# First feed-forward of a Conformer layer: one more pair of tiles by seven products, five sums by DMA, another head and another end

## The chip, the cores and the metric

The kernel runs on one core of one Trainium2 chip. The metric is the device time of one execution in microseconds (us); smaller is better. Before the change it is 2106.32 us, the median of three runs (2105.33 to 2113.24).

The engines are TensorE (PE in the profile, PEld where it loads weights), VectorE (DVE), ScalarE (ACT), GpSimd (POOL) and SyncE (SP). SP issues most of the DMA transfers; ACT and POOL issue a few. Each engine works through its own list of instructions in order.

## The reference, cut to what matters

One layer on 256 tokens of 2048 features, in float32:

```python
def swiglu_ffn(h, w_in, w_out):
    gate, up = jnp.split(h @ w_in, 2, axis=-1)
    return (jax.nn.silu(gate) * up) @ w_out
...
h = rms_norm(x, ffn1_norm[l])
x = x + MACARON_SCALE * swiglu_ffn(h, ffn1_w_in[l], ffn1_w_out[l])
# then: convolution and spatial gating, cross-attention
h = rms_norm(x, ffn2_norm[l])
x = x + MACARON_SCALE * swiglu_ffn(h, ffn2_w_in[l], ffn2_w_out[l])
return rms_norm(x, final_norm)
```

`w_in` is 2048 x 11264 (5632 gate columns and 5632 up columns), `w_out` 5632 x 2048.

## The kernel before

**Numbers in two parts.** To keep float32 accuracy, each operand of a large product is split into a high part (rounded to fp32r by a cast on ACT) and a low part (the difference, by a subtraction on DVE). A product is then three matmuls: high x high, high x low, low x high. All large matmuls are 128 x 128 x 512. A tile of weights is 128 x 1024 floats, 512 KB: `raw` as loaded, `hl` as split.

**The first feed-forward** is the class `FeedForward`. The 11264 columns of `w_in` are cut into 11 groups `j` of 512 gate and 512 up columns; a group runs over 16 tiles `k` of 128 input features. Group 0 (`run`, first loop) handles one tile after the other with 12 matmuls each (`by_two`), while x arrives: `x_arrives` loads two tiles of x, multiplies by the gain and splits (`gained`, L239 and L240), and `x_more` loads x once more by rows and squares it (`x_squares`, L525) for the root of the mean square, which `give` needs when the group ends.

Groups 1 to 10 (`group`) take the tiles in eight pairs. A pair marked "C" in `PATTERNS` takes eight products of half-tiles (`eight`: 24 matmuls). A pair marked "S" takes seven (`seven`: 21 matmuls), for which DVE first makes sums of weight halves (L388, L389, L394, L401), and the splits are those of the sums (`parts`: cast L339 on ACT, subtraction L340 on DVE). The sums on the x side (`sides`) are made once, in group 0. Before the change the pattern is "SCSCSCCC".

**Sums by DMA.** For the tiles listed in `SUMMED` (2, 7 and 13 of each group) DVE does not subtract. `summed` lets ACT write minus the high part into the low half of a buffer (L358), then the high part (L359), and POOL issues a DMA that loads the weights a second time and adds them to that low half (L360):

```python
nc.scalar.activation(out=hl[:, 1], in_=raw, func=AF.Copy, scale=-1.0)
nc.scalar.copy(out=hl[:, 0], in_=raw)
nc.gpsimd.dma_start(out=hl[:, 1], in_=self.w_in[j, :, k], accum_op=ALU.add)
```

There are two such buffers in the first feed-forward, used by turns: `hl_s`, and the second half of `more` (which lies where x lay, and is there from the end of group 0). The buffer for the sum after next is refilled right after a summed tile has been used, so a refill begins when TensorE has read the low half for the last time (L289 reads it) and must have landed when TensorE reads it next. In the second feed-forward there is one buffer, `hl_s`.

**Order.** The program is written in one order and a scheduler with a model of times sets the order on each engine; the matmuls of neighbouring tiles stand interleaved there. A DMA is issued when its buffer is free; nine raw buffers go round (`raw`).

**The end.** The last 512 columns of the output are added, squared (`add_up`) and scaled by the inverse root (`give`), token half by token half, and stored.

Of the kernel before, what the change touches and what calls it, by code (L numbers as in the profile page):

```python
# [36 lines left out]
PATTERNS = ("SCSCSCCC", "SCSCSCCC")  # L37

SUMMED = ((2, 7, 13), (2, 7, 13))
# [3 lines left out]
    ("ffn1_norm", KD), ("mix_norm", KD), ("xattn_norm", KD), ("mem_norm", KD), ("ffn2_norm", KD),  # L43
# [23 lines left out]
def layer(ctx: ExitStack, tc: tile.TileContext, a: dict):  # L67
# [118 lines left out]
    nc.vector.memset(ones, 1.0)  # L186
    nc.scalar.activation(out=st.tile([P, 1], F32, name="warm"), in_=ones[:, 0:1], func=AF.Silu)
    ident = const.tile([P, P], F32, name="ident")
    make_identity(nc, ident)
    pv = const.tile([P, NPV], F32, name="pv")  # L190
    xt = ctx.enter_context(tc.tile_pool(name="xt", bufs=1))
    xT = xt.tile([P, KD, T], F32, name="xT", tag="x")
# [44 lines left out]
    def gained(dst, k, x, g):  # L237

        nc.scalar.activation(out=dst[:, k, 0], in_=x, func=AF.Copy, scale=g)  # L239
        nc.vector.scalar_tensor_tensor(  # L240
            out=dst[:, k, 1], in0=x, scalar=g, in1=dst[:, k, 0].bitcast(F32), op0=ALU.mult, op1=ALU.subtract
        )

# [55 lines left out]
    class FeedForward:  # L299
# [62 lines left out]
        def sides(self, i):  # L362
# [4 lines left out]
            for q in range(2):  # L367
                nc.scalar.activation(out=xg[:, q], in_=xT[:, k + q], func=AF.Copy, scale=col(self.gain, k + q))
# [55 lines left out]
        def group(self, j, r, after=()):  # L424
# [10 lines left out]
            for p, c in enumerate(self.pattern):  # L435
# [8 lines left out]
                else:  # L444
                    late = p > self.spairs[-1] and len(after) > 0
                    self.eight(j, p, b, p == self.pattern.index("C"), p == n - 1, late)
                    if p > self.spairs[-1] + 1:
# [7 lines left out]
        def run(self, before, after, root, more=None):  # L455
# [3 lines left out]
            for k in range(KD):  # L459
                before(k)  # L460
                w = self.parts(self.raw(0, k))
# [3 lines left out]
                if k == 13:  # L465
                    r = root()
                    nc.scalar.activation(out=st.tile([P, 1], F32, name="warm"), in_=ones[:, 0:1], func=AF.Silu)
                    self.summed(0)
            if more is not None:
                more()  # L470
                self.summed(1)
            self.give(0, [acc[t][0] for t in range(2)], [acc[t][1] for t in range(2)], r)
            turns = [self.turn(i) for i in range(2 * NG)]
            for j in range(1, NG):
                if j < NG - 1:
                    self.group(j, r)
                else:
                    now, turns = turns[:4], turns[4:]
# [40 lines left out]
    head = PV["mix_norm"][0]  # L519

    def x_squares(c):

        raw = wraw.tile([P, 1024], F32, name="raw")
# [3 lines left out]
    with ExitStack() as stack:  # L527
        ff = FeedForward(stack, ("S1", "S0", "S2"), x_hl, "ffn1_norm", a["ffn1_w_in"], PATTERNS[0], SUMMED[0])

        def x_arrives(k):  # L530
            if k % 2 == 0:
                nc.sync.dma_start(out=xT[:, k:k + 2], in_=a["xT"][:, k:k + 2])
            if k == 0:
                nc.sync.dma_start(out=pv[:, :head], in_=a["pv"][:, :head])
            gained(x_hl, k, xT[:, k], col("ffn1_norm", k))

        def x_more(k):
            if k == 6:
                nc.sync.dma_start(out=pv[:, head:], in_=a["pv"][:, head:])
            if k in (5, 7, 9, 11):  # L540
                x_squares(k // 2 - 2)
            if k in (6, 9, 12):
# [13 lines left out]
        turns = ff.run(x_arrives, x_more, x_root, x_given)  # L556
# [588 lines left out]
```

## Time and profile before

| what | value |
|---|---|
| median of three runs | 2106.32 us |
| the profiled execution: its own time | 2108.84 us |
| the profiled execution: span from first to last instruction | 2107.0 us |
| mean granted TensorE clock | 0.998 |
| TensorE busy | 2084.5 us, 99% of the span, 9764 matmuls |
| DVE busy | 1576.8 us, 75% |
| ACT busy | 1161.6 us, 55% |
| first matmul starts | 7.11 us |
| first matmul of group 1 | 57.53 us |
| first matmul of the down projection | 475.06 us |

Read a row of the timeline so: start, duration, engine, line of the kernel, operation, output<-inputs; in brackets how long the engine sat idle before it, and what ended that. Matmuls overlap (one lasts 0.39 us, but they follow each other every 0.23 us), so the pace is a stretch divided by its matmuls.

### The profile page before, as it was taken

The page shows a single profiled execution, that of the slowest core. Times are in us where ns is not written, and L with a number is a line of the kernel's source. Part 1 is how long each engine was busy: PE and PEld are TensorE (multiplying, and loading weights), DVE is VectorE, ACT ScalarE, POOL GpSimd, SP SyncE. Part 2 cuts the span into 40 slices and gives each one's busy share as a digit, 9 for nine tenths or more (in the row PEclk, how much of TensorE's full clock was granted, in tenths as well). Part 3 has the DMA queues.
Part 4 walks back from the last instruction along what each step waited for, and adds up shares of the span by engine and source line. Part 5 has one row for each costly group of instructions (what it writes and reads, how often), then busy time and mean ns, then how long its engine had stood idle before and what let it go on. Part 6 is the DMA issues. An engine that isn't in the chain of part 4 may idle for free.

```text
span 2107.0 us, 26590 instructions
## 1 busy us (share of the span) xinstructions
PE 2084.5 (99%) x9764; PEld 1738.5 (83%) x9764; DVE 1576.8 (75%) x2215; ACT 1161.6 (55%) x1450; POOL 67.7 (3%) x83
## 2 busy tenths in 40 slices
PE   8999999999999999999999999999999999999998
PEld 6888888888888888888888888888888888888886
DVE  6888888876655589889877665777888887787754
ACT  7666566645544454445665454556665666554443
POOL 0000000000000000000000000000000000000000
PEclk9999999999999999999999999999999999999999
DMA  9778777855666676666565543686787778556664
GB/s 360 230 227 257 229 238 245 263 167 169 216 198 188 206 236 200 190 176 185 176 201 185 186 154 111 206 281 191 231 259 247 232 229 250 178 160 202 197 192 149
DMA packets 122244, 442.34 MB, mean 210 GB/s; under 512 B 13697, under 2 KB 13825, under 8 KB 121729
## 3 DMA queue, kind: packets, MB, share of 16 engines
q1 hardware_dynamic: 113184, 407.35, 58.8%
q0 software_dynamic: 8640, 32.51, 8.5%
q8 instruction: 76, 1.25, 0.2%
q10 hardware_dynamic: 288, 0.79, 0.1%
q14 instruction: 56, 0.45, 0.1%
HBM read 438.49 MB, written 2.10 MB: 209 GB/s over the span
## 4 chain that ended last, share of the span: by engine, by line
PE 84%; issue 11%; DMA 2%; ACT 1%; POOL 1%; DVE 1%; SPq 0%; POOLq 0%; ACTq 0%
PE acc L172 12%; PE acc L173 12%; PE acc L171 12%; PE acc L125 9%; PE acc L289 7%; PE acc L288 7%; PE acc L291 7%; PE acc L126 4%; PE acc L277 2%; PE acc L276 2%; PE acc L275 2%; PE aux L263 1%; PE acc L1066 1%; PE acc L1065 1%; PE acc L1067 1%
## 5 line engine op out<-in xcount | busy, mean ns | idle before, releaser
L113 DVE TENSOR_TENSOR hl<-raw,hl 128x1024 fp32r<-128x1024 f32 (+1 forms) x402 | 488.6, 1216 | 282.5 <-ACT hl L112 281.1
L112 ACT CAST hl<-raw 128x1024 fp32r<-128x1024 f32 (+1 forms) x402 | 419.7, 1045 | 481.6 <-PE acc L173 289.3
L339 ACT CAST hl<-spare 128x1024 fp32r<-128x1024 f32 (+1 forms) x135 | 131.8, 993 | 95.5 <-DVE spare L389 38.5
L340 DVE TENSOR_TENSOR hl<-spare,hl 128x1024 fp32r<-128x1024 f32 (+1 forms) x135 | 154.4, 1150 | 35.8 <-ACT hl L339 34.2
L288 PE MATMUL acc<-hl,x_hl 128*128 128x512 f32 x408 | 144.2, 394 | 9.7 <-ACT hl L339 9.7
L289 PE MATMUL acc<-hl,x_hl 128*128 128x512 f32 x408 | 149.9, 395 | 0.0
L340 DVE TENSOR_TENSOR hl<-raw,hl 128x1024 fp32r<-128x1024 f32 (+1 forms) x101 | 113.9, 1131 | 45.9 <-ACT hl L339 44.3
L339 ACT CAST ring<-spare 128x1024 fp32r<-128x1024 f32 (+1 forms) x99 | 97.2, 988 | 68.9 <-DVE spare L389 26.9
L340 DVE TENSOR_TENSOR ring<-spare,ring 128x1024 fp32r<-128x1024 f32 (+1 forms) x99 | 112.9, 1145 | 19.9 <-ACT ring L339 18.8
L291 PE MATMUL acc<-hl,x_hl 128*128 128x512 f32 x408 | 127.5, 392 | 0.0
L339 ACT CAST hl<-raw 128x1024 fp32r<-128x1024 f32 (+1 forms) x101 | 97.7, 977 | 51.8 <-PE acc L291 16.1
L172 PE MATMUL acc<-hl,x_hl 128*128 128x512 f32 x256 | 100.5, 392 | 0.2 <-DVE hl L113 0.2
L172 PE MATMUL acc<-hl,m_hl 128*128 128x512 f32 x256 | 100.4, 392 | 0.0
L173 PE MATMUL acc<-hl,m_hl 128*128 128x512 f32 x256 | 100.2, 391 | 0.0
L173 PE MATMUL acc<-hl,x_hl 128*128 128x512 f32 x256 | 99.8, 390 | 0.0
L288 PEld LDWEIGHTS acc<-hl,x_hl 128*128 128x128 f32 x408 | 76.8, 189 | 25.9 <-ACT hl L339 10.1
L289 PE MATMUL acc<-ring,x_hl 128*128 128x512 f32 x248 | 93.1, 389 | 0.0
L288 PE MATMUL acc<-ring,x_hl 128*128 128x512 f32 x248 | 91.2, 390 | 0.0
L171 PE MATMUL acc<-hl,m_hl 128*128 128x512 f32 x256 | 91.2, 393 | 0.0
L289 PEld LDWEIGHTS acc<-hl,x_hl 128*128 128x128 f32 x408 | 77.2, 190 | 16.9 <-DVE hl L340 1.1
L291 PEld LDWEIGHTS acc<-hl,x_hl 128*128 128x128 f32 x408 | 77.5, 190 | 16.4
L125 PE MATMUL acc<-x_hl,hl 128*128 128x512 f32 x256 | 91.0, 398 | 0.0
(359 smaller groups left out, 5173.9 us busy)
## 6 DMA issues: line engine op xcount, KB each, us to landing
spare<-in_ffn_w_in SPq DMA_DIRECT2D x192, 512.0 KB, 6.4
raw<-in_ffn_w_out SPq DMA_DIRECT2D x176, 512.0 KB, 3.8
raw<-in_ffn_w_in SPq DMA_DIRECT2D x160, 512.0 KB, 6.3
hl_s<-in_ffn_w_in POOLq DMA_DIRECT2D x44, 512.0 KB, 7.3
raw<-in_w_mix_vg SPq DMA_DIRECT2D x32, 512.0 KB, 4.6
raw<-in_w_k SPq DMA_DIRECT2D x32, 512.0 KB, 4.0
raw<-in_w_v SPq DMA_DIRECT2D x32, 512.0 KB, 4.4
raw<-in_w_mix_out SPq DMA_DIRECT2D x32, 512.0 KB, 4.6
```

What stands on the lines that cost most here:

```text
L112: nc.scalar.copy(out=hl[:, 0, :size], in_=raw[:, :size])
L113: newest[0] = nc.vector.tensor_tensor(out=hl[:, 1, :size], in0=raw[:, :size], in1=hl[:, 0, :size].bitcast(F32), op=ALU.subtract)
L125: nc.tensor.matmul(acc, lhsT=w_hi, rhs=x_hl, start=first, stop=False, skip_group_check=True)
L126: nc.tensor.matmul(acc[:, 0], lhsT=w_lo, rhs=x_hl[:, 0], start=False, stop=last, skip_group_check=True)
L171: nc.tensor.matmul(acc[t], lhsT=x[:, 0, s], rhs=hi[:, k], start=k0 + k == 0, stop=False)
L172: nc.tensor.matmul(acc[t], lhsT=x[:, 0, s], rhs=lo[:, k], start=False, stop=False)
L173: nc.tensor.matmul(acc[t], lhsT=x[:, 1, s], rhs=hi[:, k], start=False, stop=k0 + k == nk - 1)
L288: nc.tensor.matmul(acc[t][g], lhsT=x[:, 0, s], rhs=hi[:, cols[g]], start=(t, g) in first, stop=False)
L289: nc.tensor.matmul(acc[t][g], lhsT=x[:, 0, s], rhs=lo[:, cols[g]], start=False, stop=False)
L291: nc.tensor.matmul(acc[t][g], lhsT=x[:, 1, s], rhs=hi[:, cols[g]], start=False, stop=last)
L339: nc.scalar.copy(out=hl[:, 0, :n], in_=raw[:, :n])
L340: newest[0] = nc.vector.tensor_tensor(out=hl[:, 1, :n], in0=raw[:, :n], in1=hl[:, 0, :n].bitcast(F32), op=ALU.subtract)
```

## The change

1. In the first feed-forward the pattern becomes "SCSCSCSC": pair 6 (tiles 12 and 13) goes by seven products. The summed tiles become 2, 6, 7, 11, 14; in the last group those below 14.
2. The head: the gain and tile 0 of x are one array (`gains_x0`), loaded with tile 1 of x from ACT's queue; the first weights come in two halves from SP (`early`) and are split half by half; 11 matmuls of ones by ones (`WARM`) precede the first real one. The rows of x go to `h` tiles that are still unused (not to `raw` buffers) and are asked for after tiles 2, 4, 6, 8 instead of 5, 7, 9, 11. The other constants (`pv`) come in one load.
3. `give(0)` is written ahead of `more()`. Of the turns of `h` for the down projection two stand in the last group instead of four.
4. The end: the sum of the first three squares is made ahead (`most`), so that `give` needs no reduction, and one operation with two scalars from a tile replaces a scalar_tensor_tensor.

```diff
-PATTERNS = ("SCSCSCCC", "SCSCSCCC")
-SUMMED = ((2, 7, 13), (2, 7, 13))
+PATTERNS = ("SCSCSCSC", "SCSCSCCC")
+SUMMED = ((2, 6, 7, 11, 14), (2, 7, 13))
+WARM = 11
...
+    gx = xt.tile([P, KD + KD * T], F32, name="gx", tag="x")
+    gains, xT = gx[:, :KD], gx[:, KD:].rearrange("p (k t) -> p k t", t=T)
+    nc.scalar.dma_start(out=gx[:, :KD + T], in_=a["gains_x0"])
+    nc.scalar.dma_start(out=xT[:, 1], in_=a["xT"][:, 1])
+    nc.vector.memset(ones, 1.0)
+    idle = pa.tile([P, 2, T], F32, name="aux")
+    for _ in range(WARM):
+        nc.tensor.matmul(idle[:, 0, :P], lhsT=ones, rhs=ones, start=True, stop=True)
...
+        def early(self, before):
+            self.raw_at += 1
+            self.at += 1
+            raw = wraw.tile([P, 1024], F32, name="raw")
+            hl = whl.tile([P, 2, 1024], F32R, name="hl")
+            halves = [slice(G, 2 * G), slice(0, G)]
+            for s in halves:
+                nc.sync.dma_start(out=raw[:, s], in_=self.w_in[0, :, 0, s])
+            x = before(0)
+            for s in halves:
+                with tc.issue_after(x.ins):
+                    split(hl[:, 0, s], hl[:, 1, s], raw[:, s])
+            return hl
...
+            self.give(0, [acc[t][0] for t in range(2)], [acc[t][1] for t in range(2)], r)
             if more is not None:
                 more()
                 self.summed(1)
-            self.give(0, [acc[t][0] for t in range(2)], [acc[t][1] for t in range(2)], r)
...
-                    now, turns = turns[:4], turns[4:]
+                    at = 2 * self.pattern[-2:].count("C")
+                    now, turns = turns[:at], turns[at:]
...
-        raw = wraw.tile([P, 1024], F32, name="raw")
+        raw = ff.h[7 - c].rearrange("p a b -> p (a b)")
...
-            if k in (5, 7, 9, 11):
-                x_squares(k // 2 - 2)
-            if k in (6, 9, 12):
+            if k in (2, 4, 6, 8):
+                x_squares(k // 2 - 1)
+            if k in (6, 9, 12, 15):
                 ff.sides(k // 3 - 2)
...
-            nc.vector.reduce_sum(out=tot, in_=sums[:, t], axis=AX.X)
-            nc.scalar.activation(out=s, in_=tot, func=AF.Sqrt, scale=1.0 / D, bias=eps)
+            nc.scalar.activation(out=s, in_=last, func=AF.Sqrt, scale=1.0 / D, bias=most[t])
...
-            nc.vector.scalar_tensor_tensor(out=r, in0=v, scalar=r, in1=s, op0=ALU.mult, op1=ALU.add)
+            nc.vector.tensor_scalar(out=r, in0=v, scalar1=r, scalar2=s, op0=ALU.mult, op1=ALU.add)
```

What this does to the order is seen at three places. In these rows `acc` and `aux` are accumulators, `hl`, `ring`, `more` and `hl_s` buffers of split weights, `x_hl` the split x.

**ACT at the start.** Before, ACT begins with its table and then waits for SP's loads of `xT` and `pv`:

```order
L187 ACT_TABLE_LOAD
L187 ACTIVATE warm<-ones 128x1
L467 ACTIVATE warm<-ones 128x1 x2
L239 ACTIVATE x_hl<-xT,pv 128x256 x2
L368 ACTIVATE spare<-xT,pv 128x256 x2
L339 CAST hl<-raw 128x1024
```

Now it issues two loads itself, and the first cast is of half a tile, after one tile of x:

```order
L196 DMA gx<-in_gains_x 128x272
L197 DMA gx<-in_xT 128x256
L204 ACT_TABLE_LOAD
L204 ACTIVATE warm<-ones 128x1
L499 ACTIVATE warm<-ones 128x1
L252 ACTIVATE x_hl<-gx 128x256
L123 CAST hl<-raw 128x512
```

Two tiles of x and two extra copies of x that stood ahead of the first cast have moved behind it.

**TensorE in a late group, from the last use of `hl_s` to its next.** The low half is read by L289 (before) and L303 (now). Before, the last reads of one content of `hl_s` and what follows:

```order
L289 MATMUL acc<-hl_s,x_hl 128x512
L288 MATMUL acc<-hl_s,x_hl 128x512
L289 MATMUL acc<-hl_s,x_hl 128x512
L291 MATMUL acc<-hl_s,x_hl 128x512 x2
L288 MATMUL acc<-ring,x_hl 128x512
```

and the first reads of the next content, 115 matmuls after the last L289 above:

```order
L291 MATMUL acc<-ring,x_hl 128x512 x2
L288 MATMUL acc<-hl_s,x_hl 128x512
L289 MATMUL acc<-hl_s,x_hl 128x512
L288 MATMUL acc<-hl_s,x_hl 128x512
L289 MATMUL acc<-hl_s,x_hl 128x512
```

Now, at about the same group, the last read of the low half:

```order
L302 MATMUL acc<-hl_s,x_hl 128x512
L303 MATMUL acc<-hl_s,x_hl 128x512
L305 MATMUL acc<-hl_s,x_hl 128x512
L302 MATMUL acc<-ring,x_hl 128x512
L303 MATMUL acc<-ring,x_hl 128x512
```

and the first read of the next content of the low half, 28 matmuls later:

```order
L302 MATMUL acc<-hl_s,x_hl 128x512 x3
L289 MATMUL acc<-ring 128x512
L289 MATMUL aux<-ring 128x512
L289 MATMUL acc<-hl,x_hl 128x512
L303 MATMUL acc<-hl_s,x_hl 128x512 x2
```

The two uses of one buffer have moved from 115 matmuls apart to 28.

**ACT in the same groups.** Before, two refills follow each other with seven casts between them:

```order
L358 ACTIVATE hl_s<-spare 128x1024
L359 CAST hl_s<-spare 128x1024
L339 CAST hl<-spare 128x512
L339 CAST ring<-spare 128x1024
L339 CAST more<-raw 128x1024
L339 CAST hl<-raw 128x1024
L339 CAST hl<-raw 128x512
L339 CAST hl<-raw 128x1024
L339 CAST ring<-spare 128x1024
L358 ACTIVATE more<-raw 128x1024
L359 CAST more<-raw 128x1024
```

Now three refills (two of `more`, one of `hl_s` between them) stand within twelve rows:

```order
L372 ACTIVATE more<-spare 128x1024
L373 CAST more<-spare 128x1024
L353 CAST ring<-raw 128x512
L432 ACTIVATE h_129<-spare,r_x_109 128x512
L353 CAST more<-raw 128x1024
L372 ACTIVATE hl_s<-spare 128x1024
L373 CAST hl_s<-spare 128x1024
L353 CAST hl<-spare 128x1024
L432 ACTIVATE h_129<-spare,r_x_109 128x512
L353 CAST hl<-spare 128x1024 x2
L372 ACTIVATE more<-raw 128x1024
L373 CAST more<-raw 128x1024
```

The refills, which were spread evenly, now come close together.

Over the program there are 8430 matmuls of 512 columns instead of 8460, and 49 refills in the first feed-forward instead of 29.

More of the change, by code (lines that the diff above doesn't have):

```diff
@@ L554, in x_given @@
             ff.hls.append(more[:, 2:])
-        turns = ff.run(x_arrives, x_more, x_root, x_given)
+        turns = ff.run(x_arrives, x_more, x_root, x_given, early=True)
         xT = xt.tile([P, KD, T], F32, name="xT", tag="x")
@@ L1050, in layer @@
         finish()
+        most = [st.tile([P, 1], F32, name=f"f_most{t}") for t in range(2)]
+        for t in range(2):
+            nc.vector.reduce_sum(out=most[t], in_=sums[:, t, 0:3], axis=AX.X)
+            nc.vector.tensor_scalar(
+                out=most[t], in0=most[t], scalar1=1.0 / D, scalar2=RMS_EPS, op0=ALU.mult, op1=ALU.add
+            )
         warm = nc.scalar.activation(out=st.tile([P, 1], F32, name="warm"), in_=ones[:, 0:1], func=AF.Sqrt)
```

45 lines of the change are left out of this document (22 added, 23 removed).

## The prediction

> **What bounds the kernel now.** I read the page's busy times first, then the busy times of three stretches of the first feed-forward, then the timeline where TensorE waits.
>
> ```profile
> PE 2084.5 (99%) x9764; PEld 1738.5 (83%) x9764; DVE 1576.8 (75%) x2215; ACT 1161.6 (55%) x1450; POOL 67.7 (3%) x83
> PE 84%; issue 11%; DMA 2%; ACT 1%; POOL 1%; DVE 1%; SPq 0%; POOLq 0%; ACTq 0%
> 0.00:7.11 7.11, 0.00 (x1) 0.00 (x1) 2.16 (x9) 4.69 (x10) 0.70 (x6) 1.00 0.72 220
> 7.11:57.53 50.42, 47.84 (x193) 38.40 (x193) 33.74 (x53) 37.08 (x54) 1.88 (x2) 0.97 0.96 358
> 57.53:474.80 417.27, 416.80 (x1844) 344.65 (x1843) 341.76 (x408) 250.81 (x278) 24.62 (x29) 1.00 0.74 233
> ```
>
> The page: TensorE is busy all the time. The stretches (columns: window, length, busy and count of PE, PEld, DVE, ACT, POOL, granted clock, DMA share, GB/s) are the time before the first matmul, group 0, and groups 1 to 10. In the third TensorE stands still for 0.47 of 417 us and makes a matmul every 416.80 / 1844 = 0.226 us. So a matmul less is 0.226 us less, and a wait is a full loss.
>
> **Matmuls.** Ten groups lose 24 - 21 = 3 matmuls each: 30 x 0.226 = 6.8 us gained, if the others keep up. Per group of 180 matmuls (40.7 us) they must do this (groups of instructions from 102 to 430 us, and the DMA queues with packets, MB and share of 16 engines from 100 to 420 us):
>
> ```profile
> L388 DVE TENSOR_TENSOR spare<-raw 128x512 f32<-128x512 f32 x12 | 8.2, 687 | 5.2 <-DMA raw<-in_ffn_w_in 5.2
> L340 DVE TENSOR_TENSOR hl<-spare,hl 128x1024 fp32r<-128x1024 f32 (+1 forms) x44 | 50.2, 1149 | 9.2 <-ACT hl L339 8.7
> L358 ACT ACTIVATE hl_s<-spare 128x1024 fp32r<-128x1024 f32 x7 | 7.4, 1059 | 7.0 <-PE acc L289 7.0
> L359 ACT CAST hl_s<-spare 128x1024 fp32r<-128x1024 f32 x7 | 7.2, 1033 | 0.0
> q1 hardware_dynamic: 18085, 65.86, 55.4%
> q0 software_dynamic: 3387, 12.30, 21.7%
> ```
>
> DVE: one pair by seven more is four sums of 0.687 and four subtractions of 1.149 (7.3 us); of plain tiles there are 3 instead of 7 (4 x 1.149 = 4.6 us less). Before, DVE was busy 341.76 / 417.27 = 82%, 33.9 of 41.4 us; now 36.6 of 40.7, 90%. ACT: four casts more, four less, and two refills more of 1.059 + 1.033: 24.9 + 4.2 = 29.1 of 40.7 us, 72%. DMA: an ordinary tile takes 0.554 x 320 / 65.86 x 0.524 = 1.41 us of all 16 engines, an adding one 0.217 x 320 / 12.30 x 0.524 = 2.96. So 16 x 1.41 + 3 x 2.96 = 31.4 us per group become 37.4 of 40.7 us, 92%. All of it fits, with TensorE as cover; if that is gone, DVE is the next bound at 36.6 us.
>
> **Head.** Three losses are in the trace:
>
> ```profile
> 0.84 0.17 DVE L186 MEMSET ones<- 128x128 f32 x1 [0.84 <-PEq L1135]
> 1.65 0.90 SPq L349 DMA_DIRECT2D raw<-in_ffn_w_in  x2
> 3.83 0.91 ACT L239 ACTIVATE x_hl<-xT,pv 128x256 fp32r<-128x256 f32 x2 [1.13 <-DMA pv<-in_pv]
> 6.01 1.04 ACT L339 CAST hl<-raw 128x1024 fp32r<-128x1024 f32 x1 [0.47 <-DMA raw<-in_ffn_w_in]
> 7.11 2.07 PE L288 MATMUL acc<-hl,x_hl 128*128 128x512 f32 x4 [7.11 <-ACT hl L339]
> 11.50 0.62 PE L291 MATMUL acc<-hl,x_hl 128*128 128x512 f32 x2
> 11.96 0.39 PE L288 MATMUL acc<-hl,x_hl 128*128 128x512 f32 x1
> 30.12 0.33 SPq L524 DMA_DIRECT2D raw<-in_x  x1
> 42.69 1.06 ACT L525 ACTIVATE raw<-raw 128x1024 f32<-128x1024 f32 x1 [1.92 <-DMA raw<-in_x]
> 44.82 1.50 PE L288 MATMUL acc<-hl,x_hl 128*128 128x512 f32 x4 [2.58 <-ACT hl L339]
> 49.34 0.39 PE L288 MATMUL acc<-ring,x_hl 128*128 128x512 f32 x1
> 874.50 0.64 PEld L774 LDWEIGHTS aux<-wT,vs 128*128 128x128 f32 x4
> 875.06 0.19 PEld L172 LDWEIGHTS acc<-hl,m_hl 128*128 128x128 f32 x1
> ```
>
> The first matmul waits until 7.11 for a cast of a whole tile whose load was the third in SP's queue (1.65). The 12 matmuls from 7.11 to 11.96 take 4.85 us instead of 2.7: they run slowly at first, and 2.1 us are lost. At 42.24 TensorE stops for 2.58 us, because ACT, in order, waits for the last rows of x (asked for at 30.12, there at 42.69); and then the 12 matmuls from 44.82 take 4.52 instead of 2.7 us, so 1.8 more. In all group 0 has 192 x 0.226 = 43.4 us of work and ends at 57.53.
>
> After the change the weights are first in SP's queue and in halves, x comes through ACT's, and the x rows are asked for three tiles earlier into free tiles, so that the stop at 42 goes. Before, 0.79 MB had to come, issued by 2.1, and were there at 6.01; now it is 0.40 MB, issued some 0.9 us earlier and 1.1 us shorter at 358 GB/s: there at 4.0, and with one product of x (half of 0.91) and half a cast (0.52) ready at 5.1. The 11 matmuls of ones are two passes each; four such passes took 0.56 us at full clock (874.50 to 875.06), so 0.28 us each, and 0.5 by the slow pace (4.85 / 2.7 as long): begun at 1.05, when the ones are there, eight of them fill the 4.4 us that the slow pace lasted before (7.11 to 11.50), three more end at about 6.1, and TensorE, in order, begins there with an open clock. 6.1 + 43.4 is 49.5; 0.5 us for small waits (DMA at 96% stays the bound of this stretch) gives 50.0: 7.5 us gained. Bounds: 4.4 (only the stop goes), 8.5 (start at 5.1). What the moved x rows push back is the weights of tiles 3 to 9, by 0.5 MB each time; TensorE needs 2.7 us per tile, and a tile with its sixteenth of both copies of x is 0.79 MB, 2.2 us at 358 GB/s, so I cost that at nothing.
>
> **End.**
>
> ```profile
> 2097.26 0.75 DVE L1039 TENSOR_SCALAR spare<-spare,f_r 128x1024 f32<-128x1024 f32 x1
> 2097.93 0.68 DVE L1015 SCALAR_TENSOR_TENSOR spare<-acc,spare 128x512 f32<-128x512 f32 x1
> 2099.40 0.16 DVE L1025 TENSOR_REDUCE f_tot<-sums 128x1 f32<-128x4 f32 x1 [0.79 <-ACT sq L1019]
> 2099.59 0.15 DVE L1027 TENSOR_SCALAR f_v<-f_tot 128x1 f32<-128x1 f32 x1
> 2100.11 0.60 DVE L1029 SCALAR_TENSOR_TENSOR f_r<-f_v,f_r,f_s 128x1 f32<-128x1 f32 x1
> ```
>
> The reduction (0.19 to the next start) goes and 0.60 becomes the 0.15 of L1027: 0.64 us. The first token half has the same gain, and the second half's L1015 stood right behind the first half's scaling L1039 on DVE, so some 0.5 more: 1.1 us, between 0.6 and 1.3. Two turns moved behind the last group have 12 matmuls (2.7 us) or more between transpose and use, for a cast and a subtraction of half the size of L359 and L340 (1.1 us); at nothing. `give(0)` ahead of `more()` and the single load of `pv` touch nothing that is late; at nothing.
>
> **The refills** are the term that speaks against the change. The second feed-forward shows one whole, and the longest that TensorE waited for (then the landings of the DMA view: second feed-forward, first, first, and `hl_s` from 100 to 240 us):
>
> ```profile
> 1728.37 0.39 PE L289 MATMUL acc<-hl_s,x_hl 128*128 128x512 f32 x1
> 1728.79 1.06 ACT L358 ACTIVATE hl_s<-spare 128x1024 fp32r<-128x1024 f32 x1 [1.17 <-PE acc L289]
> 1730.26 0.89 POOL L360 DMA_DIRECT2D hl_s<-in_ffn_w_in  x1 [12.06 <-ACT hl_s L358]
> 1739.22 0.50 PE L289 MATMUL acc<-hl_s,x_hl 128*128 128x512 f32 x1 [0.72 <-DMA hl_s<-in_ffn_w_in]
> hl_s<-in_ffn_w_in POOLq DMA_DIRECT2D x28, 512.0 KB, 7.3
> hl_s<-in_ffn_w_in POOLq DMA_DIRECT2D x11, 512.0 KB, 8.3
> more<-in_ffn_w_in POOLq DMA_DIRECT2D x12, 512.0 KB, 8.2
> DMA to landing us min/median/max: 5.3/8.3/9.3
> ```
>
> From the last read (1728.37) to POOL's issue are 1.89 us, to the next read 10.85. So a refill takes 1.9 us plus the landing, whose medians are 7.3 us in the second feed-forward and 8.2 to 8.3 in the first ; the last row gives 5.3 to 9.3. Now count matmuls in the order between the last read of a low half and its next first read, at 0.226 us. Before, all refills of the first feed-forward have 24 us or more. After, of 47 refills 15 have less than 9.8: 6.3, 6.8, 7.0, 7.0, 7.2, 7.5 (all from tile 2 to tile 7), 8.4, five of 9.1, 9.3, 9.3, 9.7. With a landing of 7.8, between the two medians, a refill takes 9.7 us, and what is missing is 3.4 + 2.9 + 2.7 + 2.7 + 2.5 + 2.2 + 1.3 + 5 x 0.6 + 2 x 0.4 = 21.5 us. Queued behind the waiting matmul is everything, since TensorE keeps its order. With 7.3 it is 14.7 us; with 9.4 (the engines 92% busy) 49; with 5.3 it is 1.7: these are the ends. I take 7.8, because the neighbours in the first feed-forward landed in 8.2, while TensorE's own waits lighten the DMA.
>
> **The clock after a wait.** The 2.58 us stop was followed by 1.8 us of slow matmuls, the 0.72 us wait by none that shows. Six of the waits above are of 2.2 to 3.4 us: 0 to 10.8 us; I take half, 5.4. The Trainium skill ("TensorE: Matmul & The Clock Gate", Part 1, "HAM oscillation") has the rule that only gaps above about 3.4 us throttle the array; this trace disagrees, with 2.58. By that rule the sum below would be 5.4 us lower.
>
> **Sum.** From the execution profiled: 2108.8 - 6.8 - 7.5 - 1.1 + 21.5 + 5.4 = 2120.3. The median of the runs lies 2.5 under that execution, so 2117.8: **2118 us**, 0.55% slower. About 0.5% (10.5 us) is what a measurement of this kernel can tell from no change.
>
> **Rivals.**
> (1) The refills land in time, under 4.4 us after the issue, and nothing waits: 2106.3 - 15.4 = 2091, faster. For it: SP's loads are fewer while TensorE waits, and the shortest landing was 5.3, which already leaves only 1.7 us. Against it: medians of 7.3 and more. It decides below a landing of 6. The Trainium skill ("DMA: Bandwidth & Descriptors", "Anatomy of one DMA", the GpSimd path) has a fit of 2.0 us plus bytes over 436e3 per us; for 512 KB that would be an estimate of 3.2 us and this rival. The rows above, with an adding DMA beside loads, don't agree.
> (2) Half of it: landing 7.3, no slow clock: 2106.3 - 15.4 + 14.7 = 2106, no change. For it: the second feed-forward, with distances down to 9.7, has only that one wait of 0.72.
> (3) The DMA engines become the bound at 92%: landings of 9.4, 49 us of waits and slow matmuls after a dozen of them (another 11): 2106.3 - 15.4 + 60 = 2151.
>
> **Chances.** My forecast (2110 to 2130) 0.52, of which 0.17 lie under 2117; (1) 0.18; (2) 0.22; (3) 0.08. So faster by over 0.5% (under 2095.8) 0.18, within 0.5% 0.39, slower 0.43. The range 2090 to 2134 takes in (1), (2) and the forecast's own and leaves (3) out.
>
> **What would show it.** In the profile after: the first real matmul near 6 us and the first of group 1 near 50; no stop at 42; in groups 1 to 10 TensorE waiting for DMAs of `hl_s` and `more` at L303, some 15 times, about once a group for 2 to 3.5 us, with slow matmuls behind. Groups 1 to 10 would then last 417.3 - 6.8 + 27 = 437 us. I am wrong if those waits are not there (landings under 6 us), if DVE or ACT is what TensorE waits for, or if the clock stays open throughout.

## The result, and the profile after

The changed kernel takes 2144.6 us (median of 4 runs, 2143.7 to 2145.8), the kernel before 2106.5 beside it: ratio 1.0179, 95% interval 1.0167 to 1.0192. The change makes it 1.8% slower, 38 us; I had forecast 12 us slower, with 2134 us as the upper end. The profiled execution took 2145.8 us, with a span of 2144.0.

First the same three stretches as before the change (window, length, busy and count of PE, PEld, DVE, ACT, POOL, granted clock, DMA share, GB/s): up to the first real matmul, group 0, groups 1 to 10.

```profile
0.00:5.77 5.77, 4.71 (x22) 4.71 (x23) 1.02 (x3) 3.11 (x7) 0.70 (x6) 1.00 0.65 221
5.77:49.59 43.82, 43.82 (x194) 36.19 (x194) 35.77 (x64) 39.40 (x62) 1.89 (x2) 1.00 1.03 386
49.59:506.71 457.12, 430.15 (x1809) 343.22 (x1808) 357.05 (x447) 281.87 (x318) 42.06 (x49) 0.98 0.81 237
```

Group 1 begins at 49.59 instead of 57.53, 7.9 us earlier: the head does what it should. But groups 1 to 10 last 457.1 instead of 417.3 us, with 30 matmuls fewer: TensorE stands still for 457.12 - 430.15 = 27.0 us (0.5 before), and its matmuls are slower. What it waits for in that stretch (microseconds in all, times, longest):

```profile
PE acc L303 <- DMA more<-in_ffn_w_in: 10.4, 4, 4.4
PE acc L289 <- DVE spare L466: 6.9, 5, 5.4
PE acc L303 <- DMA hl_s<-in_ffn_w_in: 6.4, 5, 2.2
PE aux L289 <- DVE spare L456: 2.3, 2, 1.2
```

16.8 us are refills, nine of them; 9.2 us are DVE's sums of finished accumulators, for which TensorE never waited before. One refill from the timeline: last read of `more`'s sum at 384.15, ACT's negation, POOL's issue, then the first four products of the new sum (they read the high half, which is there) and the first that needs the low half:

```profile
384.15 0.40 PE L305 MATMUL acc<-more,x_hl 128*128 128x512 f32 x1
385.06 1.06 ACT L372 ACTIVATE more<-spare 128x1024 fp32r<-128x1024 f32 x1
386.52 0.89 POOL L374 DMA_DIRECT2D more<-in_ffn_w_in  x1 [15.97 <-ACT more L372]
389.49 1.10 PE L302 MATMUL acc<-more,x_hl 128*128 128x512 f32 x4
395.49 1.22 PE L303 MATMUL acc<-more,x_hl 128*128 128x512 f32 x2 [4.44 <-DMA more<-in_ffn_w_in]
```

2.4 us to the issue and 9.0 from there to the landing, 4.44 of it waited for. And the longest wait is none of these. DVE stood 4.87 us at the first sum of a seven-product pair because its raw weights were not there; L466, which TensorE needs, was queued behind it:

```profile
279.26 0.69 DVE L402 TENSOR_TENSOR spare<-raw 128x512 f32<-128x512 f32 x1 [4.87 <-DMA raw<-in_ffn_w_in]
280.48 1.28 DVE L466 TENSOR_TENSOR spare<-spare,acc 128x512 f32<-128x512 f32 x2
281.21 0.80 PE L289 MATMUL acc<-ring,x_hl 128*128 128x512 f32 x1 [5.42 <-DVE spare L466]
```

The DMA view of 262 to 282 us shows where the raw weights were (a digit per 0.5 us, the busy tenths of the 16 engines; then three of the kinds of issue in it):

```profile
DMA  9999999910657996559999999999999999999942
spare<-in_ffn_w_in SPq DMA_DIRECT2D x4, 512.0 KB, 8.4
more<-in_ffn_w_in POOLq DMA_DIRECT2D x1, 512.0 KB, 8.8
raw<-in_ffn_w_in SPq DMA_DIRECT2D x1, 512.0 KB, 10.6
```

The engines lie nearly idle from 266 to 267 us, after SP has waited 5.6 us for DVE to free a raw tile, are half to nearly full up to 271, and then full for 10 us on end, in which they move 284 GB/s (416 from 264 to 266, as full). The raw tile asked for at 268.68 lands after 10.6 us instead of 6.5 (the stage's median). So the ordinary weights are late as well, not only the refills.

After a wait the matmuls are slow for a while. Behind 1.81 us of waiting the first four go on quickly, eight from 163.10 on follow each other every 0.43 us, and from 166.48 it is 0.23 again. The granted clock says why: it is the third number from the right in the last two rows below, which are of two of those stretches.

```profile
162.03 0.73 PE L303 MATMUL acc<-hl_s,x_hl 128*128 128x512 f32 x2 [1.81 <-DMA hl_s<-in_ffn_w_in]
...
163.10 0.63 PE L303 MATMUL acc<-hl_s,x_hl 128*128 128x512 f32 x1
163.53 0.63 PE L305 MATMUL acc<-hl_s,x_hl 128*128 128x512 f32 x1
163.95 0.63 PE L289 MATMUL acc<-more,x_hl 128*128 128x512 f32 x1
...
166.48 0.40 PE L290 MATMUL acc<-more,ring 128*128 128x512 f32 x1
166.71 0.40 PE L291 MATMUL acc<-more,ring 128*128 128x512 f32 x1
```

```profile
163.10:166.48 3.38, 3.38 (x10) 2.64 (x8) 0.00 (x0) 0.00 (x0) 0.00 (x0) 0.51 1.02 417
166.48:170.00 3.52, 3.52 (x17) 2.85 (x16) 1.27 (x2) 2.35 (x3) 0.00 (x0) 1.00 0.06 22
```

The trace's record of the clock has five such stretches at half clock in groups 1 to 10, four of 3.41 us and one of twice that, and all five begin at whole multiples of 3.413 us after the clock first rose. Over the stage, the matmul intervals over 0.27 us hold 14.0 us more than at 0.2265 each (worked out from all its rows). What is left, some 6 us, is a steady interval of 0.231 instead of 0.227 us, from the first group on; and the rest of the program, whose code is the same but for two turns of `h`, takes 6.5 us more in the same manner (1628.1 us from the first matmul of L174 to the last matmul, 1621.6 before). The end gained what was expected: 9.2 us from the last matmul's start to the end of the span instead of 10.4.

### The profile page after: what moved, and what is told of

It reads as the page before. It is cut to its first block, busy times and chain, and to the rows that moved or that the text cites. A ratio compares the mean times of both kernels' runs of the same rounds, so it can differ in the third digit from the quotient of the medians.

```text
span 2144.0 us, 26698 instructions
## 1 busy us (share of the span) xinstructions
PE 2105.8 (98%) x9756; PEld 1741.1 (81%) x9756; DVE 1594.1 (74%) x2262; ACT 1193.9 (56%) x1494; POOL 85.1 (4%) x103
## 4 chain that ended last, share of the span: by engine, by line
PE 79%; issue 16%; DMA 2%; POOL 2%; ACT 1%; DVE 0%; POOLq 0%; DVEq 0%; ACTq 0%
PE acc L176 12%; PE acc L175 12%; PE acc L174 12%; PE acc L128 8%; PE acc L303 6%; PE acc L305 6%; PE acc L302 6%; PE acc L129 4%; PE acc L290 2%; PE acc L291 2%; PE acc L289 2%; PE aux L277 1%; DMA spare<-in_ffn_w_in 1%; PE acc L1100 1%; PE acc L1101 1%
## 5 line engine op out<-in xcount | busy, mean ns | idle before, releaser
L116 DVE TENSOR_TENSOR hl<-raw,hl 128x1024 fp32r<-128x1024 f32 (+1 forms) x402 | 488.7, 1216 | 283.0 <-ACT hl L115 282.1
L115 ACT CAST hl<-raw 128x1024 fp32r<-128x1024 f32 (+1 forms) x402 | 419.4, 1045 | 486.4 <-PE acc L176 302.2
L354 DVE TENSOR_TENSOR hl<-raw,hl 128x1024 fp32r<-128x1024 f32 (+1 forms) x95 | 105.0, 1110 | 35.4 <-ACT hl L353 34.9
L303 PE MATMUL acc<-hl,x_hl 128*128 128x512 f32 x324 | 115.7, 391 | 0.0
L353 ACT CAST hl<-raw 128x1024 fp32r<-128x1024 f32 (+1 forms) x95 | 89.7, 959 | 44.8 <-DVE raw L415 14.2
L374 POOL DMA_DIRECT2D hl_s<-in_ffn_w_in x54 | 47.1, 873 | 1200.1 <-ACT hl_s L372 1200.1
L174 PE MATMUL acc<-hl,m_hl 128*128 128x512 f32 x256 | 91.3, 393 | 0.0
L128 PE MATMUL acc<-y_hl,hl 128*128 128x512 f32 x256 | 90.5, 399 | 0.0
L174 PE MATMUL acc<-hl,x_hl 128*128 128x512 f32 x256 | 90.0, 392 | 0.0
L303 PE MATMUL acc<-hl_s,x_hl 128*128 128x512 f32 x216 | 83.2, 400 | 6.8 <-DMA hl_s<-in_ffn_w_in 6.8
L128 PE MATMUL acc<-o_hl,hl 128*128 128x512 f32 x256 | 89.2, 393 | 0.0
```

Source lines behind the costliest of these rows:

```text
L115: nc.scalar.copy(out=hl[:, 0, :size], in_=raw[:, :size])
L116: newest[0] = nc.vector.tensor_tensor(out=hl[:, 1, :size], in0=raw[:, :size], in1=hl[:, 0, :size].bitcast(F32), op=ALU.subtract)
L128: nc.tensor.matmul(acc, lhsT=w_hi, rhs=x_hl, start=first, stop=False, skip_group_check=True)
L174: nc.tensor.matmul(acc[t], lhsT=x[:, 0, s], rhs=hi[:, k], start=k0 + k == 0, stop=False)
L303: nc.tensor.matmul(acc[t][g], lhsT=x[:, 0, s], rhs=lo[:, cols[g]], start=False, stop=False)
L353: nc.scalar.copy(out=hl[:, 0, :n], in_=raw[:, :n])
```

## The experiments

Lengths of groups 1 to 10, from the first matmul of group 1 to the first of the output projection; idle is TensorE's in that stretch; times are medians. Stage, idle and DMA share are of one profiled execution each, which lay up to 3.9 us under the median (three_sums) and, in three_buffers, 9.6 us above it (2168.0 us):

```
version (first feed-forward)            stage   idle   DMA    time
before: 3 pairs by seven, 3 sums        417.5    0.5   0.74   2106.8
head_ends: as before, new head/ends     419.3    0.5   0.75   2108.6
head_ends_8k: + placement as before     417.5    0.5   0.75   2101.1
the change: 4 pairs, 5 sums             457.1   27.0   0.81   2144.6
aligned: + 64-byte starts               455.6   29.3   0.82   2145.3
after_8k: + placement as before         457.4   30.6   0.81   2137.7
no_sub5: after_8k, less work on DVE     455.9   29.6   0.82   2140.4
plain_copy: refills without adding      423.0    7.2   0.75   2113.3
ring_five: ring of 5                    468.2   35.6   0.80   2158.6
three_buffers: ring of 5, 3 sum tiles   473.8   34.8   0.80   2158.4
even_four: 4 sums, 8 tiles apart        432.7   13.4   0.81   2127.5
three_sums: 3 sums                      426.2   10.6   0.75   2122.3
no_sub: 3 sums, less work on DVE        414.2    2.4   0.77   2109.6
pool_sub: 3 sums, L415 on GpSimd        442.4   21.9   0.73   2125.2
```

### Where the slower pace comes from

The change makes `pv` 64 bytes shorter, adds 64 bytes ahead of x (`gx`) and drops a few small tiles, so that every large tile moved. Two runs asked whether the start addresses of the tiles matter:

```diff
# aligned: the changed kernel; before_32: the kernel before, with the same edit
-    st.tile([P, 8], F32, name="to_64")
+    st.tile([P, 16], F32, name="to_64")
```

> The changed kernel with one padding tile 32 bytes longer, so that more, gx and the summed tiles (hl_s) begin at multiples of 64 bytes as before the change; the change had left them at 32 over a multiple of 64. Theory A (the address of these tiles sets a part of TensorE's pace): the steady interval of a matmul in groups 1 to 10 falls from 0.231 to 0.227 us and that of the later stages from 0.229 to 0.227; 1809 x 0.004 + 6.5 = 14 us less, about 2130 us. Rival B (the pace comes from the load on the DMA engines or the on-chip memory, or is chance): the pace stays and so does the time, 2145 us.

> The kernel before with the same padding tile 32 bytes longer, which puts more, xT and hl_s at 32 over a multiple of 64 bytes; nothing else differs. Theory A: the interval of 0.227 us goes to about 0.230 and the time up by some 14 us, to 2120 us. Rival B: 2106.5 us as before.

`before_32` took 2118.5 us (ratio 1.0052, interval 1.0035 to 1.0068): 32 bytes of padding cost 12 us. `aligned` took 2145.3, no gain. So addresses matter, but a start at a multiple of 64 is not what was lost. The head without the pattern showed the rest:

```diff
# head_ends: the changed kernel, padded as aligned
-PATTERNS = ("SCSCSCSC", "SCSCSCCC")
+PATTERNS = ("SCSCSCCC", "SCSCSCCC")
-SUMMED = ((2, 6, 7, 11, 14), (2, 7, 13))
+SUMMED = ((2, 7, 13), (2, 7, 13))
```

> The changed kernel with the pattern and the three sums of before in the first feed-forward (and the 64-byte padding), so that only the head and the ends are changed. If the head is worth 7.9 us and the ends 1.2, as I read in the two traces, 2106.5 - 9.1 = 2097 us. If the gains of the head are given back later (a pace or waits that the new head itself brings), 2106 us or more, and the pattern is not the whole cause of the loss.

2108.6 us (1.0009, 1.0000 to 1.0018): group 1 begins at 49.5, but all later feed-forward stages are 0.4 to 0.8% longer. Taken by the weights that are read, the matmuls on `hl_s` are slow: 0.2312 us on average against 0.2272 on `more`; in the kernel before 0.2269 and 0.2266. By the order in which the program places its tiles, `hl_s` has the same address in both, and what moved by 64 bytes are the tiles ahead of it, those with x among them. So it is not a tile's own start.

The down projections, where the activation `h` takes the place of x, say more. Matmuls of weights in `hl` with `h` in `hl_s` or `hC` take 0.2333 us in head_ends and in before_32, against 0.2274 and 0.2269 in the kernel before. With `h` in `hA` or `hB` they stay within 0.2271 to 0.2279. So a matmul is slow when one of its two tiles moved against the other, whichever of the two it was. The next runs tell a start's remainder from a distance:

```diff
# head_ends_addr: head_ends with the remainders by 128 of the kernel before; hl_s 128 bytes off
+    pv = const.tile([P, NPV + 16], F32, name="pv")
+    gx = xt.tile([P, 2 * KD + KD * T], F32, name="gx", tag="x")
# head_ends_8k (and after_8k, with the change's pattern): multiples of 8192 between x_hl, ring, hl, more, hl_s
-    st.tile([P, 8], F32, name="to_64")
+    pv = const.tile([P, NPV + 16], F32, name="pv")
-            more = xt.tile([P, 4, 1024], F32R, name="more", tag="x")
+            more = xt.tile([P, KD + 4096], F32R, name="more", tag="x")[:, KD:].rearrange(...)
```

> The version with only the head and the ends changed, which took 2108.6 us instead of the expected 2097, with tiles padded so that the ring, the raw and split weights, more and hl_s begin at the same remainder by 128 bytes as in the kernel before (64; they were at 0). Theory G (the start address of the tiles sets TensorE's steady pace: 0.2275 us per matmul in that version instead of 0.2265): the pace returns to 0.2265 and the time to 2097 us. Rival H (the pace belongs to something else, the new placement in DRAM or the moved loads): 2108 us.

> Only the head and the ends changed, and tiles padded so that the summed tiles (hl_s, more) and all tiles behind them lie a multiple of 8192 bytes from the tile that holds x, as in the kernel before (the change and all versions so far moved hl_s to 32, 64 or 128 bytes beside it). In those versions the matmuls that read hl_s took 0.231 to 0.233 us each and all others about 0.2275, while in the kernel before both took 0.227. Theory I (the distance of a tile from the x tile sets the pace of its matmuls, not its own start): hl_s is back at 0.227, the 11 us that the head's gain lost are back, 2097 us. Rival H (placement in DRAM, or the moved loads): 2108 us.

> The changed kernel itself, with this same placement of the tiles. Theory I: the pace of about 0.231 us goes to 0.227 everywhere and takes 8 us of the first feed-forward and 6 to 10 of the rest with it, 2130 to 2134 us; the waits stay. Rival H: 2145 us.

`head_ends_addr`: 2108.4 us, `hl_s` at 0.232: theory G fell. `head_ends_8k`: 2101.1 us (0.9969, 0.9960 to 0.9979), 4 us above theory I's 2097, with a pace of 0.2267 on `hl_s`, `more` and the ring. Twelve matmuls on `hl_s` in the second feed-forward, with the first matmul behind them, from the timelines of before_32 (2.81 us) and of head_ends_8k (2.72):

```profile
1495.19 0.40 PE L288 MATMUL acc<-hl_s,x_hl 128*128 128x512 f32 x1
...
1498.00 0.40 PE L276 MATMUL acc<-hl,ring 128*128 128x512 f32 x1
```

```profile
1498.85 0.39 PE L301 MATMUL acc<-hl_s,x_hl 128*128 128x512 f32 x1
...
1501.57 0.39 PE L301 MATMUL acc<-hl,x_hl 128*128 128x512 f32 x1
```

`after_8k`: 2137.7 us (1.0144, 1.0128 to 1.0159), 4 us above the expected range. Placement is 6.9 of the 38 us, all of it behind the first feed-forward. That stage itself lasts 457.4 us, as long as with the slow pace: what the matmuls gained came back as waits (30.6 us of idle time instead of 27.0, and slower matmuls behind them). One more profile, of a single execution, asked how far a tile may stand off:

```diff
# off_a: the kernel before, more 256 bytes off, hl_s 384
+    xt.tile([P, 32], F32, name="gap")
-    st.tile([P, 8], F32, name="to_64")
+    st.tile([P, 72], F32, name="to_64")
```

> The kernel before with more moved by 256 bytes and hl_s by 384 (against multiples of 8192 from the tile that holds x). With 32, 64 and 128 bytes the matmuls that read the moved tile took 0.231 to 0.2335 us instead of 0.227. If the pace needs a distance of a larger power of two, both are slow (0.231 or more); if 256 bytes are enough, more is at 0.227 and hl_s slow.

`more` at 0.2268, `hl_s` at 0.2318 (332 and 177 matmuls). In these runs 256 bytes off cost nothing; 32, 64, 128 and 384 bytes cost 2 to 3% of each matmul.

### What holds the groups up

```diff
# plain_copy: the changed kernel, padded as aligned
-            nc.gpsimd.dma_start(out=hl[:, 1], in_=self.w_in[j, :, k], accum_op=ALU.add)
+            nc.gpsimd.dma_start(out=hl[:, 1], in_=self.w_in[j, :, k])
```

> The changed kernel (64-byte padding; it took 2145 us as such) with each refill of a low half as a plain copy of the same 512 KB instead of an adding one. It leaves out the addition, so the low half holds whole weights instead of the remainder; the instructions on TensorE, DVE, ACT and SP, and the distances between last and next read, are the same. An adding DMA held all 16 engines 2.96 us in the profile before, an ordinary one 1.41: five times 1.55 is 7.8 of the 40.7 us of a group less, 73% instead of 92%. Theory E (the adding DMAs fill the engines, and refills and weight loads both come late): the waits of the aligned run, 29 us with 13 us of slow matmuls, nearly all go, 2108.6 - 6.8 = 2102 to 2108 us. Theory F (DVE and ACT, in order, are the bound, and DMA waits are only where it shows): 2130 to 2145 us.

2113.3 us (1.0035, 1.0025 to 1.0046): 32 us less than aligned, 5 above theory E's range and 17 under theory F's. The stage and its DMA issues (count, KB each, median us to landing), of plain_copy and then, for comparison, the issues of the change:

```profile
49.43:472.33 422.90, 415.70 (x1808) 337.64 (x1807) 356.42 (x446) 281.74 (x318) 25.92 (x49) 1.00 0.75 254
q0 software_dynamic: 6993, 26.36, 21.3%
spare<-in_ffn_w_in SPq DMA_DIRECT2D x81, 512.0 KB, 5.0
hl_s<-in_ffn_w_in POOLq DMA_DIRECT2D x24, 512.0 KB, 6.0
more<-in_ffn_w_in POOLq DMA_DIRECT2D x23, 512.0 KB, 5.3
```

```profile
q0 software_dynamic: 7030, 26.44, 31.0%
spare<-in_ffn_w_in SPq DMA_DIRECT2D x81, 512.0 KB, 6.7
hl_s<-in_ffn_w_in POOLq DMA_DIRECT2D x24, 512.0 KB, 8.0
more<-in_ffn_w_in POOLq DMA_DIRECT2D x23, 512.0 KB, 7.3
```

Nearly the same bytes in the same queue hold the engines 21.3% of 422.9 us instead of 31.0% of 457.1: 90 us against 142, 5.2 us per group. Refills land 2 us earlier, and SP's ordinary loads 1.7 us, though nothing was done to them: the adding DMAs slow what runs beside them. It is not the share alone that does so. In the kernel before, with three adding sums and a share of 0.74, the same loads landed in 6.4 us; here, at 0.75, in 5.0. The next two ask for the distance alone, with the engines' work left as it is:

```diff
# ring_five: aligned, without the ring's third place
-            ff.ring.append(more[:, :2])
# three_buffers: that place is a third tile for sums
-            ff.ring.append(more[:, :2])
-            ff.hls.append(more[:, 2:])
+            ff.hls += [more[:, :2], more[:, 2:]]
```

> The changed kernel (with the 64-byte padding), the same five sums by DMA and the same seven-product pairs, so the same work on DVE and DMA engines per group, but three tiles for the sums instead of two: the tile that served as third place of the ring of split weights becomes the third, so a summed tile is refilled 8 to 11 tiles ahead instead of 5 to 8, and split weights rotate over 5 tiles instead of 6. Theory C (the distance between the last read and the next read is the cause of the waits, and of those of DVE and the raw tiles behind them): no wait for a DMA of a sum, and 2106.5 - 9.1 - 6.8 = 2091 us. Rival D (DVE and the DMA engines, 90% and 92% busy, are the bound): waits of the same 27 us at other places, 2130 us or what the aligned version takes. A ring of five that is too short would show as waits for ACT's or DVE's split of a tile.

> The changed kernel (64-byte padding, 2145 us) with split weights that rotate over five tiles instead of six; sums and their two tiles as in the change. It is the control for the version with three tiles for the sums, which took 2158 us with this ring. If the ring of five costs 13 us or more by itself (2158 us and more), that run could not show what the distance is worth. If it costs under 4 us (2145 to 2149), distance was not the cause, since with 8 to 11 tiles of it the time did not fall.

2158.4 and 2158.6 us. The ring of five costs 13 us by itself, so `three_buffers` can be read only against `ring_five`, not against the change: with 8 to 11 tiles of distance instead of 5 to 8, TensorE hardly waits for refills any more (24.6 us of ring_five's waits in the stage, 3.2 here), and the median is the same. TensorE's waits for refills in ring_five:

```profile
PE acc L303 <- DMA hl_s<-in_ffn_w_in: 15.3, 6, 4.9
PE acc L303 <- DMA more<-in_ffn_w_in: 9.3, 5, 3.4
```

What came in their place, in three_buffers, for TensorE and then for DVE:

```profile
PE acc L289 <- ACT ring L353: 8.1, 3, 4.2
PE acc L289 <- DVE spare L466: 7.5, 3, 3.0
PE acc L290 <- DVE ring L354: 3.8, 5, 1.2
```

```profile
DVE spare L402 <- DMA spare<-in_ffn_w_in: 26.4, 7, 6.3
DVE spare L403 <- DMA raw<-in_ffn_w_in: 11.4, 4, 4.0
DVE spare L402 <- DMA raw<-in_ffn_w_in: 8.6, 3, 4.6
```

DVE waits 52.7 us in all for raw weights here, 35.6 in ring_five: the lateness went from the refills to them. That this is the DMA engines' doing fits `plain_copy`, but these two runs do not show it by themselves, and a third tile beside a ring of six was not tried. The last question with five sums is DVE's load:

```diff
# no_sub5: after_8k, first feed-forward only
-            nc.vector.tensor_tensor(out=two[:, lo], in0=two[:, lo], in1=one[:, lo], op=ALU.subtract)
```

> The changed kernel with its five sums by DMA and the tiles placed as before (2137.7 us), without the fourth sum of each seven-product pair in the first feed-forward (L415), so the fourth product reads a wrong operand. DVE has 2.8 of 35.7 us less to do in a group; the DMA engines, ACT, distances and TensorE's work are the same. Theory E (with five sums the adding DMAs are the first bound, DVE the second): the waits for refills stay (about 20 us and the slow matmuls behind them), only those for DVE go: 2122 to 2132 us. Theory F (DVE is the first bound and the DMA waits only follow from it): most of the 47 us of losses go, 2100 to 2112 us.

2140.4 us (1.0162, 1.0145 to 1.0178): nothing gained, where theory E had expected 2122 to 2132 and theory F still less:

```profile
49.81:505.71 455.90, 426.35 (x1809) 344.36 (x1807) 334.86 (x407) 285.46 (x318) 42.05 (x49) 0.97 0.82 239
```

DVE fell from 357.0 to 334.9 us busy, and the stage lasts 455.9. The change itself, aligned, after_8k and no_sub5 differ in pace and in DVE's work and have the same stage, 455.6 to 457.4 us, at a DMA share of 0.81 to 0.82. Of the versions with five sums only `plain_copy`, which takes work off the DMA engines, shortened it.

### Whether the pattern could gain with fewer sums

```diff
# even_four, three_sums: aligned, with
-SUMMED = ((2, 6, 7, 11, 14), (2, 7, 13))
+SUMMED = ((2, 6, 10, 14), (2, 7, 13))      # even_four
+SUMMED = ((2, 7, 11), (2, 7, 13))          # three_sums
# no_sub: three_sums without L415, as no_sub5
# pool_sub: three_sums, placed as after_8k, L415 (L414 there) by nc.gpsimd
```

> The changed kernel (64-byte padding) with four sums by DMA per group, at tiles 2, 6, 10 and 14, so that each of the two tiles is refilled eight tiles ahead; by the order of instructions the shortest distance is 9.3 us instead of 6.3. The fifth sum goes back to DVE and ACT (1.15 us on DVE, one cast instead of two passes on ACT). DVE then has 37.7 of 40.7 us of work per group, the DMA engines 34.4. Theory E (DMA engines, at 92% with five sums and 85% with four) and theory C (distance): most waits go, 2108.6 - 6.8 = 2102 to 2110 us. Theory F (DVE is the bound, 93%): 2145 us or more.

> The changed kernel (64-byte padding) with three sums by DMA per group, at tiles 2, 7 and 11 (distances 15 us and more). DVE then has 38.9 of 40.7 us of work per group, 96%; the DMA engines 31.4, 77%. Theory E or C: no wait for a refill, about 2102 us unless DVE takes over. Theory F: more waits for DVE than with four or five sums, 2145 us or more. If three sums are slower than four, DVE is a bound of its own at 38.9; if faster, it is not.

> The version with three sums at tiles 2, 7 and 11 (2122 us) without the fourth sum of each seven-product pair in the first feed-forward (L415), so the fourth product reads a wrong operand; DVE has 4 x 0.69 = 2.8 us less in each group, 36.1 instead of 38.9 of 40.7 us, all else is the same. Theory F (DVE's load is what is left as the bound once the refills are no longer waited for): the 10 us of waits and 7 us of slow matmuls of that version nearly go, about 2108 us. Rival J (it is the order of ACT's work, or raw tiles that come late): under 4 us less, 2118 us or more.

> A whole kernel again: four pairs by seven products, three sums at tiles 2, 7 and 11, tiles placed as before, and L415 on GpSimd instead of DVE. Leaving L415 out took the three-sum version from 2122 to 2109.6 us, and the placement is worth 7.5: 2102 us if GpSimd's operation (1.78 us for this size in the profile before, against 0.69) is hidden and GpSimd's own queue, in which the refills' DMAs are issued and wait for ACT, does not hold it up. If it is held up there, the fourth product comes late in every pair: 2110 to 2130 us.

even_four 2127.5 us (1.0099, 1.0080 to 1.0119), three_sums 2122.3 (1.0070, 1.0055 to 1.0086), no_sub 2109.6 (1.0010, 1.0001 to 1.0019), pool_sub 2125.2 (1.0089, 1.0074 to 1.0104). Each sum less is faster, but even_four and three_sums both lie between what the theories expected, and three_sums still needs 426.2 us for the stage, 7 more than head_ends with its 30 matmuls more. There TensorE waits for DVE's and ACT's splits:

```profile
PE acc L290 <- DVE hl L354: 3.1, 2, 1.7
PE acc L289 <- ACT ring L353: 2.3, 2, 1.4
PE acc L289 <- DVE spare L466: 1.9, 1, 1.9
```

DVE is busy 375.0 of 426.2 us, 88%. Taking 2.8 us per group off it (no_sub) removes most of the waits (2.4 us of idle time instead of 10.6), and the stage then is 414.2, 5.1 us under head_ends: only there does a gain from the 30 matmuls appear. The time is theory F's (2108 expected, 2109.6 measured). By the rule written before three_sums, its being faster than even_four would have cleared DVE; no_sub contradicts that rule. But no_sub also takes a step out of the chain that each fourth product waits for, so DVE's load and the length of that chain are not told apart. Putting the same subtraction on GpSimd gave nothing: it takes 2.0 us there (0.69 on DVE), and beside it the largest group of DVE's own subtractions into the ring grew from 1.22 (no_sub) to 1.33 us on average:

```profile
L414 POOL TENSOR_TENSOR spare<-spare 128x512 f32<-128x512 f32 x17 | 33.9, 1996 | 123.4 <-DVE hl L353 51.0 <-DVE ring L353 26.2 <-DVE more L353 20.8
L353 DVE TENSOR_TENSOR ring<-spare,ring 128x1024 fp32r<-128x1024 f32 x34 | 45.0, 1331 | 5.1 <-ACT ring L352 5.0
```

The Trainium skill ("SBUF — State Buffer", "SBUF: two separate sides") has DVE and GpSimd share a pair of ports, held for a whole instruction, where the DVE operation reads two inputs from SBUF and the GpSimd one reads SBUF; this trace agrees. The 27 of DVE's subtractions of 128x1024 that overlap one of GpSimd's took 1.50 us on average, up to 2.32, and the other 141 took 1.22.

The version to keep is head_ends_8k, the new head and ends with the old pattern and the tiles where they were: 0.31% under the kernel before.

## Why the prediction was wrong

Against the profiled execution I had 2120.3 us, and it took 2145.8; the sign was right, the size was not.

- **Head: right.** 7.5 us forecast, 7.9 measured; first real matmul at 5.77 (forecast near 6), group 1 at 49.59 (near 50). It holds by itself: head_ends_8k has all other stages within 1.3 us of before.
- **End: right.** 1.1 forecast, 1.2 measured. Moving two turns, costed at nothing, cost 1.4 us (the output projection lasts 250.3 us in after_8k, 248.9 in head_ends_8k).
- **Matmuls: right in number, never earned.** The 6.8 us are in the count, but every version that does all of the pattern's work has a longer stage than before.
- **Refill waits: 21.5 forecast, 16.8 measured.** They are at L303, nine instead of fifteen, from 0.3 to 4.4 us, with landings of 8.0 and 7.3 us (7.8 forecast). So the place and the size were near, and the reason was half of it: with a ring of five, three_buffers removed them and the time stayed.
- **The step that failed** is "All of it fits, with TensorE as cover", said of DMA engines at 37.4 of 40.7 us. They did those 37 us of work per group (0.81 x 45.7), but in 45.7 us. No version got more than 0.82 out of them in this stage. I counted 92% as room. The view of 262 to 282 us shows what becomes of the room: empty for a moment while the raw tiles are all taken, then full, with every transfer late. TensorE then waits for DVE's sums too, which come late behind the raw weights: 27.0 us of idle time, nearly 10 more than the refills and the 0.5 of before, the largest single wait among them, and a wait for DVE was on my own list of signs that I am wrong. Of the 38 us, plain_copy gives back 32 by making the same transfers lighter. My rival (3), the DMA engines as the bound, was the right mechanism, and I gave it 0.08. That its 2151 us come near the time is partly luck: it had 49 us of waits and landings of 9.4, where 27.0 and 8.0 were measured, and it knew nothing of the slower steady pace (6.1 us here and 6.5 in the rest).
- **The clock: mis-sized.** 5.4 us forecast, 14.0 measured. I charged six waits of over 2.2 us; the rows above show eight slow matmuls behind 1.81. In the versions with five adding sums and a ring of six, slow matmuls come to 0.44 to 0.58 of the waiting time (14.0 to 27.0; 13 to 29.3 in aligned; 17.3 to 30.6 in after_8k; 17.1 to 29.6 in no_sub5). The Trainium skill's bound of about 3.4 us for such gaps ("TensorE: Matmul & The Clock Gate", Part 1, "HAM oscillation"), cited in the prediction, is not what these runs show.
- **Placement: not seen.** The diff shows `pv` shrinking and `gx` growing, and I read neither as a change of address: 6.9 us of the 38.

In order, on the profiled executions: head and end 0.5 us better than forecast; groups 1 to 10 457.1 instead of 437.4, that is refills -4.7, other waits +9.7, slow matmuls +8.6 and the steady pace +6.1; the rest of the program +6.5, mostly by placement. Together 25.7, where 25.5 were missing. The 6.1 are an item of this list and not a cause: after_8k has the old pace and a stage just as long.

What stays open: how the 82% comes about, whether a longer ring or more raw tiles would raise it, whether the adding DMAs hurt by their share or by what they do to the transfers beside them, and what in the chip makes a distance of 256 bytes different from 128.

## What to carry to other kernels

Add up the DMA engines' time per stage by what each kind of transfer holds them (an adding one here twice an ordinary one), and where the sum comes near the length of the stage (92% here) and buffers are few, treat them as the bound. Here, with five adding sums, neither a longer distance (three_buffers against ring_five) nor less work on DVE (no_sub5 against after_8k) nor a faster pace of the matmuls (after_8k against the change) gained anything in the stage. Charge TensorE's waits there about one and a half times, for the slow matmuls behind them. And when a diff resizes a small tile, compare the addresses of the large ones before and after.

## What the runs showed of the hardware

- Matmuls of 128x512 fp32r whose two tiles lie a multiple of 8192 bytes from each other, or 256 bytes beside one, followed each other every 0.2267 us; with 32 bytes off it was 0.2335, with 64 0.2312, with 128 or 384 0.232 (weights in `hl_s` or `more`, x in the other tile). In the down projections, with the moved tile on the other side, they were slow too (0.232 to 0.233). The Trainium skill ("SBUF — State Buffer", "Operand start alignment") asks that an operand start at a multiple of its element size and says of this rule that it is about legality, not speed; all starts here keep it, and 32 bytes still cost 12 us.
- An adding DMA of 512 KB held the engines 1.6 times as long as a plain one in the same queue (142 against 90 us for 7030 and 6993 packets), and ordinary transfers beside it landed in 6.7 instead of 5.0 us.
- Behind a wait of 1.81 us, eight matmuls ran at 0.43 us each, from the fifth on: a drop of the clock needs less than the 2.58 us of waiting seen before. Where the wait falls decides. In the 17 traces of this case the clock is halved 41 times after the first 20 us, always on a grid of 3.413 us. Behind all 36 steps of that grid in which TensorE, at full clock, had waited 1.81 us or more, the next step had half the clock; behind the other 10,301 it was so five times, with 1.31 to 1.80 us of waiting. (Worked out from the clock and the waits of all traces.)
